# Modulation of a two-layer diffusion backbone on one core: four feature blocks in TensorE's four column tiles, and gate rows through DRAM

## The chip, the cores and the metric

One core of a Trainium2 chip runs the whole program. The metric is the device time of one execution in microseconds, the median of several runs of one build. One execution was also recorded by the hardware profiler, and all rows below come from it.

## The reference, cut to what matters

384 tokens (128 context, 256 latent) of width 1024 go through two layers. Each layer makes six modulation vectors of 1024 for each of two conditioning vectors (context and latent):

```python
def _modulation(cond, w, b):
    m = (jax.nn.silu(cond) @ w + b)[:, None, :]     # w: 1024 x 6144
    return jnp.split(m, 6, axis=-1)

def _layer(x, cond, attend, p, ffn):
    shift_a, scale_a, gate_a, shift_f, scale_f, gate_f = _modulation(cond, p['ada_w'], p['ada_b'])
    h = _ln_plain(x) * (1 + scale_a) + shift_a
    mix, k, v = _token_mixers(h, attend, p)
    x = _ln_affine(DEEPNORM_ALPHA * x + gate_a * mix, p['ln1_g'], p['ln1_b'])
    h = _ln_plain(x) * (1 + scale_f) + shift_f
    x = _ln_affine(DEEPNORM_ALPHA * x + gate_f * ffn(h), p['ln2_g'], p['ln2_b'])
    return x, k, v
```

The mixers are `h @ w_in` (1024 x 2048), attention, a gated convolution and a chunk MLP, then `@ w_out`. The FFN is a dense SwiGLU of width 2816 in layer 0 and the two best of eight experts in layer 1. All is float32.

## The kernel before, in words

Tokens are three tiles of 128. Dense products split both operands into two fp32r parts and make three fp32r matmuls for each 128 of the contraction. Weights arrive by DMA from SyncE's queue in units of 1 MB into five buffers named `st`, and are split by ScalarE (`CAST q<-st`) and VectorE (`TENSOR_TENSOR q<-st,q`) into the buffers `wh` and `wl`. `w_in` comes in four quarters of 512 columns.

A planner (`Plan`) records every operation and then writes each engine's order by itself: it always takes the ready operation with the earliest estimated start, and among those that could start at once the one that the program names first, inside a window of 380 operations. So the order in the text is a priority, not the order of execution. Buffers are given out by tag, in the text's order within a tag. PSUM has eight banks: at most three `pd` (dense sums), two `py` (modulation, and the output sums of the FFN) and three `pm` (transposes, attention). When the plan leaves TensorE idle long enough, `keep_warm` adds matmuls on the identity. `matmuls` records several matmuls as one operation, which the planner can't part.

The modulation of one block `nb` of 512 features (12 a layer; shift_a is 0 and 1, scale_a 2 and 3, gate_a 4 and 5, shift_f 6 and 7, scale_f 8 and 9, gate_f 10 and 11) is `ada_rows`: two units of `ada_w`, each four fp32 matmuls of 128 contraction rows with 32 output columns (two used, the conditioning vectors) in the four column tiles of TensorE. Column tile j holds the sum over contraction blocks j and 4 + j, so rows 32j and 32j + 1 of the bank hold a quarter of the sum. The bank is copied to fp32r `eh` and the rest `el`, and matmuls with a selection matrix add the four quarters: `ada_cols` turns them into feature columns (eight matmuls with `selc`, 128x2), `ada_bcast` into two tiles that hold a row on all 128 partitions (four matmuls with `selb`, 128x512, for the gates), and `ada_dram` into a row that goes to DRAM (two matmuls with `selc` as stationary operand), from where `spread` fetches it for the routing and the end.

The fills lie between the quarters of `w_in` in `mixers` (`fill(0)` to `fill(3)`) and between the two halves of an FFN step (`fill(n)`). Layer 0 makes blocks 0 to 3 at the start, 6 to 9 in fills 0 to 2 (one, one, two blocks), 4 and 5 before the last attention tile, 10 and 11 in FFN steps 2 and 3, and layer 1's 0 to 3 in FFN steps 1 to 4. Layer 1 makes 6 to 11 in fills 0 to 2 and 4 and 5 at the same place.

Of the kernel before, what the change touches and what calls it, by code (L numbers as in the profile page):

```python
# [10 lines left out]
F32 = mybir.dt.float32  # L11
# [9 lines left out]
P = 128  # L21
D = 1024
NT = 3
KC = 8
# [10 lines left out]
FILL0 = ((0,),(1,),(2,3),())  # L35
GATE = 1
# [9 lines left out]
FILL2 = ((0,1), (2,3), (4,5), (), ())  # L46
# [197 lines left out]
class Plan:  # L244
# [36 lines left out]
    def record(self, eng, name, a, k, others=(), more=()):  # L281
# [15 lines left out]
        for b, _ in more:  # L297
            outs.append(b[0])
            ins += b[1:]
# [34 lines left out]
        if more:  # L334
            op.alts[eng] = (name, a, k, self.price(eng, name, outs, list(a[1:]), a, k) + sum(self.price(eng, name, [b[0]], list(b[1:]), b, q) for b, q in more))
# [62 lines left out]
    def flush(self):  # L398
# [85 lines left out]
        for o in order:  # L484
            if not isinstance(o, Op):
                o()
                continue
            a = [x.real() if isinstance(x, (View, Later)) else x for x in o.args]
            if o.name == "call":
                a[0](*a[1:], **{q: v.real() for q, v in o.kw.items()})  # L490
                continue
            k = {q: (x.real() if isinstance(x, View) else x) for q, x in o.kw.items()}
            getattr(self.real[o.eng], o.name)(*a, **k)  # L493
            for b, q in o.more:
                getattr(self.real[o.eng], o.name)(*[x.real() for x in b], **q)  # L495
# [80 lines left out]
class Net:  # L576
    def __init__(self, ctx, nc, tc, A, O):
        self.bnc, self.tc, self.A, self.O = nc, tc, A, O
        self.nc = Plan(nc)
        self.n = 0  # L580
        self.part = ''
        ep = ctx.enter_context
        self.const = ep(tc.tile_pool(name="const", bufs=1))
        sb = ep(tc.tile_pool(name="sb", bufs=1))
        ps = ep(tc.tile_pool(name="ps", bufs=1, space=PSUM))
        self.pools = {}
        dr = ep(tc.tile_pool(name="dr", bufs=1, space=bass.MemoryType.DRAM))
        for pool, name, elems, cap in (
            (dr, "dr", NT * D, dict(dr=1)),
            (dr, "md", 6 * 512, dict(md=1)),  # L590
            (sb, "st", 2048, dict(st=5)),
            (sb, "q4", 1024, dict(x=3, a4=12, wh=6, wl=6)),
            (sb, "q2", 512, dict(m2=21, e2=3)),
            (sb, "q1", 24, dict(s=47)),
            (ps, "bank", 512, dict(pd=3, py=2, pm=3)),
        ):
            p = PPool(pool, name, elems, sum(cap.values()), cap, pool is ps)
            p.cap.update(CAPS.get(name, {}))
            for k in cap:
                self.pools[k] = p  # L600
# [48 lines left out]
    def setup(self):  # L649
# [14 lines left out]
        self.selc = const([2], F32R, "selc")  # L664
        idv = self.idf.rearrange("p (a b) -> p b a", b=32)
        tmp = const([2], F32, "selt")
        nc.vector.tensor_reduce(tmp, idv[:, 0:2, :], axis=AX.X, op=ALU.add)  # L667
        nc.vector.tensor_copy(self.selc, tmp)
        self.selb = const([2, P], F32R, "selb")
        for m in range(2):  # L670
            nc.vector.tensor_copy(self.selb[:, m, :], tmp[:, m : m + 1].to_broadcast([P, P]))
# [58 lines left out]
    def ada_rows(self, l, nb):  # L730
        nc = self.nc
        pa = self.bank([512], name="zrows", tag="py")
        for half in range(2):
            w = self.load(self.A["ada_w"][l, nb, half], 4, 512)
            for j in range(4):
                nc.tensor.matmul(
                    pa[32 * j : 32 * j + 32, :], self.cs[:, 4 * half + j, :], w[:, j, :],
                    start=(half == 0), stop=(half == 1), tile_position=(0, 32 * j),
                )
        eh = self.m2([512], F32R, "eh", tag="e2")  # L740
        el = self.m2([512], F32R, "el", tag="e2")
        nc.any.copy(eh, pa)
        nc.vector.tensor_sub(el, pa, eh.bitcast(F32))
        return eh, el

    def ada_cols(self, l, nb, out, one):

        nc = self.nc
        eh, el = self.ada_rows(l, nb)
        pc = self.bank([4, 2], name="zcols", tag="py")  # L750
        for j in range(4):
            s = slice(128 * j, 128 * j + 128)
            nc.tensor.matmul(pc[:, j, :], eh[:, s], self.selc, start=True, stop=False)
            nc.tensor.matmul(pc[:, j, :], el[:, s], self.selc, start=False, stop=True)
        b = self.abc[:, l, 4 * nb : 4 * nb + 4][:, :, None].to_broadcast([P, 4, 2])
        nc.vector.scalar_tensor_tensor(out, pc, one, b, op0=ALU.add, op1=ALU.add)
        return eh, el

    def ada_dram(self, l, nb, i, one, e=None):

        nc = self.nc
        b = self.m2([512], name="mrow")[0:2]
        nc.sync.dma_start(b, self.A["ada_b"][l : l + 1, 512 * nb : 512 * nb + 512].to_broadcast([2, 512]))
        eh, el = e or self.ada_rows(l, nb)
        pr = self.bank([512], name="zmrow", tag="py")[0:2]
        nc.tensor.matmul(pr, self.selc, eh, start=True, stop=False)
        nc.tensor.matmul(pr, self.selc, el, start=False, stop=True)
        nc.vector.scalar_tensor_tensor(b, pr, one, b, op0=ALU.add, op1=ALU.add)
        nc.sync.dma_start(self.mod[0:2, i, :], b)

    def spread(self, i, m, tag="m2", hold=False):
# [3 lines left out]
        self.nc.sync.dma_start(w.rearrange("p a f -> p (a f)") if n == 2 else w, self.mod[m : m + 1, i : i + n, :].rearrange("p a f -> p (a f)").to_broadcast([P, 512 * n]))  # L775
        return w

    def ada_bcast(self, l, nb, one, out=None):

        nc = self.nc  # L780
        out = out or [self.m2([512], name="mod") for m in range(2)]
        for o in out:
            nc.sync.dma_start(o, self.A["ada_b"][l : l + 1, 512 * nb : 512 * nb + 512].to_broadcast([P, 512]))
        eh, el = self.ada_rows(l, nb)
        for m in range(2):
            pb = self.bank([512], name="zbc", tag="py")
            nc.tensor.matmul(pb, self.selb[:, m, :], eh, start=True, stop=False)
            nc.tensor.matmul(pb, self.selb[:, m, :], el, start=False, stop=True)
            nc.vector.scalar_tensor_tensor(out[m], pb, one, out[m], op0=ALU.add, op1=ALU.add)
        return out  # L790
# [173 lines left out]
    def mixers(self, l, h, fill, ahead, then, ws=None):  # L964
# [66 lines left out]
        gate = lambda: [self.ada_bcast(l, 4 + nb, 0.0) for nb in range(2)]  # L1031
# [6 lines left out]
        ga = gate()  # L1038
# [72 lines left out]
    def ffn(self, l, h, fill, then):  # L1111
# [4 lines left out]
        for n, g in enumerate((5, 0, 1, 2, 3, 4)):  # L1116
# [100 lines left out]
    def route(self, mid):  # L1217

        nc = self.nc
        mods = {(i, m): self.spread(2 * i, m, "a4") for i in range(2) for m in range(2)}  # L1220
# [408 lines left out]
    def moe(self, l, mid):  # L1629
        nc, A, tc = self.nc, self.A, self.tc  # L1630
        self.pools["a4"].cap.update(**CAPS2)
        cnt = self.route(mid)
# [104 lines left out]
    def lead(self, gf, ya):  # L1737
# [4 lines left out]
        for nb in range(2):  # L1742
            gf.append([self.spread(4 + nb, m, hold=True) for m in range(2)])
# [15 lines left out]
    def body(self):  # L1759
# [47 lines left out]
        for g in range(2):  # L1807
            self.ada_cols(0, g, sh[g], 0.0)
            self.ada_cols(0, 2 + g, sc[g], 1.0)
# [3 lines left out]
        self.tables(0)  # L1813
        shf, scf = cols("shf"), cols("scf")

        def fill0(i):
            for n in FILL0[i]:
                self.ada_cols(0, 6 + n, (shf + scf)[n], n // 2)

        hf = []  # L1820
        self.mixers(0, h, fill0, lambda: None, make_h("f", scf, shf, hf), ws)
        sh, sc = cols("sh"), cols("sc")

        def fill1(g):
# [9 lines left out]
        self.mod = self.m2([6, 512], name="mod", tag="md", hold=True)  # L1834

        def fill2(i):
            for n in FILL2[i]:
                one = 1.0 if n in (2, 3) else 0.0
                e = self.ada_cols(1, 6 + n, (shb + scb)[n], one) if n < 4 else None
                self.ada_dram(1, 6 + n, n, one, e)  # L1840

        self.part = '1'
        self.mixers(1, h, fill2, lambda: self.route_prep(scb, shb), lambda t: None)
        self.moe(1, lambda: fill2(4))
# [27 lines left out]
def _layout(I):  # L1872
# [25 lines left out]
    R["ada_w"] = kblk(I["ada_w"], 2, 512)  # L1898
# [51 lines left out]
```

## Time and profile before

| what | value |
|---|---|
| median of three runs | 1175.7 us (1173.18 to 1180.41) |
| profiled execution, own time | 1172.83 us |
| its span, first to last instruction | 1171.1 us |
| mean granted TensorE clock | 0.982 |
| DMA | 282.66 MB, mean 241 GB/s |

The span lies 1.7 us inside the execution's own time, and that execution 2.9 us under the median. In the rows L493 is the one line from which the planner issues nearly all instructions (L495 for the later matmuls of a group of `matmuls`, L510 for the filler), so groups are told apart by their tiles: `st` are loaded units, `cs` the conditioning columns, `q` any SBUF buffer, `bank` any PSUM bank, `md` the DRAM rows, `dr` the routed rows in DRAM. An fp32 matmul shows as two instructions.

### The profile page before, as it was taken

Reading aid. Unit: us, or ns where it says so; the run is one execution under the profiler, and the core shown is the slowest. Engines: PE = TensorE matmul, PEld = TensorE weight load, DVE = VectorE, ACT = ScalarE, POOL = GpSimd, SP = SyncE. Lnnn points to the kernel's source line nnn. Section 1 sums busy time; section 2 is a strip of 40 time slices with the busy share of each in tenths; the row PEclk is TensorE's granted clock in tenths of the full one; section 3 lists DMA queues with packets and bytes.
Section 4 is the critical chain, followed back from the end, with each engine's and each line's share of the span. In section 5 each row is a group of like instructions: output and inputs, shape, how many; then the busy total and the mean of one; then the engine's idle time right before and its main releaser. Section 6 shows DMA issues by size and latency. Waiting matters only on the chain. (4 is left out here: it accounts for less than half of the span.)

```text
span 1171.1 us, 15554 instructions
## 1 busy us (share of the span) xinstructions
PE 1133.1 (97%) x5578; PEld 862.3 (74%) x5578; DVE 827.2 (71%) x1391; ACT 626.4 (53%) x997; POOL 124.3 (11%) x141
## 2 busy tenths in 40 slices
PE   8999999999999999989999899999999999999995
PEld 4666668877777878756666677888888888887673
DVE  4475669443535344797568877999999998987855
ACT  4545547431313223264455326878878786885652
POOL 3430003000000000055000110000000000011201
PEclk8999999999999999999999969999999999999998
DMA  9775544573839465354557436999979997996541
GB/s 375 275 267 197 166 142 143 199 269 139 328 110 332 150 238 197 149 185 156 199 186 268 163 130 224 352 362 361 345 294 347 379 361 297 366 343 245 184 176 58
DMA packets 49398, 282.66 MB, mean 241 GB/s; under 512 B 6312, under 2 KB 8104, under 8 KB 21408
## 3 DMA queue, kind: packets, MB, share of 16 engines
q1 hardware_dynamic: 47056, 275.46, 63.7%
q0 software_dynamic: 1392, 4.55, 1.1%
q10 hardware_dynamic: 864, 1.57, 0.4%
q8 instruction: 46, 0.75, 0.3%
q14 instruction: 40, 0.33, 0.1%
HBM read 278.13 MB, written 3.43 MB: 240 GB/s over the span
## 5 line engine op out<-in xcount | busy, mean ns | idle before, releaser
L493 PE MATMUL bank<-q,q 128*128 128x512 f32 (+4 forms) x4111 | 969.6, 389 | 2.6 <-DVE q L493 1.3
L493 PEld LDWEIGHTS bank<-q,q 128*128 128x128 f32 x4111 | 734.4, 189 | 196.4 <-issue 33.6
L493 DVE TENSOR_TENSOR q<-st,q 128x1024 fp32r<-128x1024 f32 x394 | 453.9, 1178 | 113.4 <-ACT q L493 89.0
L493 ACT CAST q<-st 128x1024 fp32r<-128x1024 f32 x394 | 394.0, 1016 | 196.0 <-PE bank L493 101.3
L493 DVE TENSOR_TENSOR q<-bank,q 128x512 fp32r<-128x512 f32 (+5 forms) x117 | 73.0, 635 | 70.6 <-ACT q L493 57.7
L493 DVE TENSOR_TENSOR q<-q,bank 128x512 f32<-128x512 f32 (+3 forms) x111 | 63.8, 584 | 76.7 <-PE bank L493 69.9
L493 ACT CAST q<-bank 128x512 fp32r<-128x512 f32 (+2 forms) x97 | 53.7, 562 | 103.7 <-PE bank L493 94.0
L493 ACT COPY q<-bank 128x128 f32<-128x128 f32 (+3 forms) x184 | 54.5, 350 | 76.3 <-PE bank L493 67.9
L493 PE MATMUL bank<-idf,q 128*128 128x128 f32 (+1 forms) x502 | 81.7, 287 | 12.9 <-ACT q L493 7.4
L493 POOL TENSOR_TENSOR q<-q,nhalf 128x1 f32<-128x1 f32 (+3 forms) x42 | 42.0, 1005 | 473.8 <-DVE q L493 473.7
L493 PEld LDWEIGHTS bank<-idf,q 128*128 128x128 f32 (+1 forms) x502 | 63.2, 147 | 39.5 <-ACT q L493 12.6
L493 POOL TENSOR_TENSOR q<-q,q 128x512 fp32r<-128x512 f32 (+5 forms) x69 | 61.5, 909 | 216.6 <-ACT q L493 155.0
L493 ACT ACTIVATE q<-bank 128x512 f32<-128x512 f32 (+4 forms) x57 | 29.6, 520 | 81.2 <-PE bank L493 74.4
L493 DVE TENSOR_TENSOR q<-q,q 128x512 f32<-128x512 f32 (+13 forms) x131 | 52.3, 420 | 17.4 <-POOL q L493 8.5
L493 PE MATMUL bank<-st,cs 128*32 128x512 f32 x384 | 54.8, 606 | 0.3 <-DMA st<-in_ada_w_dram 0.3
L272 POOL DMA_INDIRECT q<-dr,q x9 | 14.7, 1638 | 346.3 <-DVE q L493 346.3
L493 ACT ACTIVATE q<-bank,q 128x384 f32<-128x384 f32 (+2 forms) x62 | 33.5, 551 | 24.6 <-DVE q L493 21.5
L493 DVE TENSOR_REDUCE q<-bank 128x1 f32<-128x384 f32 (+5 forms) x64 | 24.5, 411 | 20.8 <-PE bank L495 13.5
L493 DVE SCALAR_TENSOR_TENSOR q<-q,q,q 128x512 f32<-128x512 f32 (+1 forms) x43 | 35.5, 882 | 0.1
L510 PE MATMUL bank<-idr 128*128 128x512 f32 x85 | 30.3, 500 | 1.9 <-DVE selt L667 1.7
L495 PE MATMUL bank<-q,q 64*128 64x384 f32 (+2 forms) x76 | 31.7, 515 | 0.0
L493 ACT ACTIVATE q<-bank,q,q 128x128 f32<-128x128 f32 x70 | 26.6, 467 | 4.6 <-DVE q L493 2.8
(90 smaller groups left out, 395.4 us busy)
## 6 DMA issues: line engine op xcount, KB each, us to landing
st<-in_ada_w_dram SPq DMA_DIRECT2D x48, 1024.0 KB
st<-in_moe_w2a_dram SPq DMA_DIRECT2D x40, 1024.0 KB
st<-in_moe_w1a_dram SPq DMA_DIRECT2D x32, 1024.0 KB
st<-in_moe_w3a_dram SPq DMA_DIRECT2D x32, 1024.0 KB
st<-in_ffn_w_dram SPq DMA_DIRECT2D x22, 1024.0 KB
st<-in_w_in_dram SPq DMA_DIRECT2D x16, 1024.0 KB
st<-in_moe_w1b_dram SPq DMA_DIRECT2D x16, 768.0 KB
st<-in_moe_w3b_dram SPq DMA_DIRECT2D x16, 768.0 KB
```

Source lines behind the costliest of these rows:

```text
L272: self.nc.gpsimd.indirect_dma_start(out=out, out_offset=None, in_=src.rearrange("p t d -> (p t) d"), in_offset=o)
L493: getattr(self.real[o.eng], o.name)(*a, **k)
L495: getattr(self.real[o.eng], o.name)(*[x.real() for x in b], **q)
L510: self.nc.tensor.matmul(z, a, b, start=True, stop=True)
```

## The change

The weights are laid out anew in DRAM. A group is now four feature blocks (2048 features, a third of a layer), and a unit of 1 MB is 128 contraction rows by these 2048 features. The four matmuls of a unit put the four blocks into the four column tiles, so after eight units each tile holds the whole sum of its own block, and nothing is left to add. They are recorded with `matmuls`, as one operation. Columns come from one copy of the bank to SBUF and four 128x128 transposes for a group. Rows (gates, and in layer 1 shift and scale too) are read from the bank by VectorE, two rows a block with the bias added, written to DRAM, and fetched onto all partitions by `spread`; the broadcasting matmuls are gone. The very first group (layer 0, blocks 0 to 3) differs: there two tiles hold the two halves of the contraction for a shift block and two for a scale block, so that four units suffice for each half of the features, and four fp32 matmuls with the selection matrix `selk` (128x4) make the columns.

Placing: each mixer fill 0 to 3 now takes four units in both layers, group 1 (blocks 4 to 7) in fills 0 and 1, group 2 (8 to 11) in fills 2 and 3. FFN steps 1 to 4 take two units each for layer 1's group 0, in one `py` bank that stays held from step 1 to step 4; the column bank moves to `pm` there and in the mixers. The FFN's gates are fetched in step 4, and the two blocks that FFN steps 2 and 3 held are gone from there. The numbers of units (48), of bytes and of fp32 matmuls on them stay.

```diff
...
@@ -332,7 +329,8 @@
         if more:
-            op.alts[eng] = (name, a, k, self.price(eng, name, outs, list(a[1:]), a, k) + sum(self.price(eng, name, [b[0]], list(b[1:]), b, q) for b, q in more))
+            own = lambda b: [v for v in b[1:] if isinstance(v, View)]
+            op.alts[eng] = (name, a, k, sum(self.price(eng, name, [b[0]], own(b), b, q) for b, q in [(a, k), *more]))
...
-            (dr, "md", 6 * 512, dict(md=1)),
+            (dr, "md", 12 * 512, dict(md=2)),
...
+    def ada_group(self, l, n, units, zr=None):
+        nc = self.nc
+        zr = zr or self.bank([512], name="zrows", tag="py")
+        for u in units:
+            w = self.load(self.A["ada_w"][l, n, u], 4, 512)
+            split = (l, n) == (0, 0)
+            first, last = (u % 4 == 0, u % 4 == 3) if split else (u == 0, u == KC - 1)
+            k = [4 * (j % 2) + u % 4 if split else u for j in range(4)]
+            nc.matmuls([(zr[32 * j : 32 * j + 32, :], self.cs[:, k[j], :], w[:, j, :], dict(start=first, stop=last, tile_position=(0, 32 * j))) for j in range(4)])
+        return zr
+
+    def ada_start(self, g, sh, sc):
+        nc = self.nc
+        zr = self.ada_group(0, 0, range(4 * g, 4 * g + 4))
+        e = self.m2([512], name="ae")
+        nc.any.copy(e, zr)
+        pc = self.bank([4, 2, 2], name="zcols", tag="py")
+        for c in range(4):
+            nc.tensor.matmul(pc[:, c].rearrange("p i m -> p (i m)"), e[:, 128 * c : 128 * c + 128], self.selk, start=True, stop=True)
...
+    def ada_out(self, l, n, zr, cols, rows):
+        nc = self.nc
+        if cols:
+            e = self.m2([512], name="ae")
+            nc.any.copy(e, zr)
+            pt = self.bank([4, P], name="zcols")
+            for c in range(4):
+                nc.tensor.transpose(pt[:, c, :], e[:, 128 * c : 128 * c + 128], self.idf)
+            for j, (out, one) in cols.items():
+                nb = 4 * n + j
+                b = self.abc[:, l, 4 * nb : 4 * nb + 4][:, :, None].to_broadcast([P, 4, 2])
+                nc.vector.scalar_tensor_tensor(out, pt[:, :, 32 * j : 32 * j + 2], one, b, op0=ALU.add, op1=ALU.add)
+        if rows:
+            b = self.m2([512], name="mrow")
+            for j, one in rows.items():
+                r, nb = slice(32 * j, 32 * j + 2), 4 * n + j
+                nc.sync.dma_start(b[r], self.A["ada_b"][l : l + 1, 512 * nb : 512 * nb + 512].to_broadcast([2, 512]))
+                nc.vector.scalar_tensor_tensor(b[r], zr[r], one, b[r], op0=ALU.add, op1=ALU.add)
+                nc.sync.dma_start(self.mod[l][0:2, nb, :], b[r])
...
         fill(3)
-        if GATE == 1:
-            ga = [self.ada_bcast(l, 4 + nb, 0.0) for nb in range(2)]
-            gate = lambda: ga
+        ga = [[self.spread(l, 4 + nb, m) for m in range(2)] for nb in range(2)]
         self.attend(2, qT[2], mt[2])
...
-            if n == 2:
-                gf[0] = self.ada_bcast(l, 10, 0.0)
-            elif n == 3:
-                gf[1] = self.ada_bcast(l, 11, 0.0)
+            if n == 4:
+                gf = [[self.spread(l, 10 + nb, m) for m in range(2)] for nb in range(2)]
...
+        def fill(l, sh, sc):
+            z = {}
+            def f(i):
+                if i > 3:
+                    return
+                n, us = 1 + i // 2, range(4 * (i % 2), 4 * (i % 2) + 4)
+                z[n] = self.ada_group(l, n, us, z.get(n))
+                if i == 1:
+                    self.ada_out(l, 1, z[1], {2: (sh[0], 0.0), 3: (sh[1], 0.0)}, {0: 0.0, 1: 0.0} if l == 0 else {0: 0.0, 1: 0.0, 2: 0.0, 3: 0.0})
+                if i == 3:
+                    self.ada_out(l, 2, z[2], {0: (sc[0], 1.0), 1: (sc[1], 1.0)}, {2: 0.0, 3: 0.0} if l == 0 else {0: 1.0, 1: 1.0, 2: 0.0, 3: 0.0})
+            return f
...
         def fill1(g):
             if 1 <= g <= 4:
-                self.ada_cols(1, g - 1, (sh[0], sh[1], sc[0], sc[1])[g - 1], 0.0 if g < 3 else 1.0)
+                z0[0] = self.ada_group(1, 0, (2 * g - 2, 2 * g - 1), z0[0])
+            if g == 4:
+                self.ada_out(1, 0, z0[0], {0: (sh[0], 0.0), 1: (sh[1], 0.0), 2: (sc[0], 1.0), 3: (sc[1], 1.0)}, {})
...
```

## Rows read from the trace of the kernel before

**Rows 1.** The page's first part: busy time of each engine, its share of the span and its instructions.
```profile
PE 1133.1 (97%) x5578; PEld 862.3 (74%) x5578; DVE 827.2 (71%) x1391; ACT 626.4 (53%) x997; POOL 124.3 (11%) x141
```

**Rows 2.** The table by stage: for each stretch (us from the span's start) its length, the busy time of each engine with its instructions, the granted TensorE clock as a share of 2.4 GHz, the busy share of the DMA engines, and GB/s.
```profile
60.00:180.00 120.00, 118.40 (x611) 78.71 (x612) 82.14 (x178) 57.18 (x160) 13.64 (x20) 1.00 0.51 183
180.00:480.00 300.00, 299.16 (x1462) 238.04 (x1461) 147.56 (x194) 108.82 (x146) 13.11 (x11) 1.00 0.59 213
480.00:540.00 60.00, 54.49 (x266) 39.45 (x265) 54.89 (x114) 27.92 (x61) 22.82 (x27) 1.00 0.40 141
540.00:660.00 120.00, 120.00 (x626) 79.05 (x625) 80.83 (x176) 57.55 (x157) 14.71 (x18) 1.00 0.59 213
...
660.00:690.00 30.00, 25.40 (x112) 22.56 (x111) 22.89 (x50) 11.22 (x15) 5.89 (x7) 0.71 0.29 114
```

**Rows 3.** What TensorE waited for from 150 to 480 us: engine and line, the releaser, then us in total, times, longest.
```profile
PE bank L493 <- DVE q L493: 0.4, 1, 0.4
```

**Rows 4.** TensorE's groups of instructions by form: busy us and the mean ns of one, then idle time before them.
```profile
L493 PE MATMUL bank<-selc,q 128*128 128x2 f32 x128 | 16.6, 239 | 2.0 <-ACT q L493 1.1 <-DVE q L493 0.9
...
L493 PE MATMUL bank<-q,q 128*128 128x8 f32 x48 | 10.6, 359 | 0.2 <-ACT q L493 0.2
L493 PE MATMUL bank<-q,selb 128*128 128x512 f32 x24 | 7.6, 399 | 0.0
...
L493 PE MATMUL bank<-q,selc 128*2 128x512 f32 x12 | 4.6, 400 | 1.5 <-DVE q L493 1.5
```

**Rows 5.** TensorE's instructions in order of time, neighbours of one form merged: start, us, engine, line, operation, out and in, count, and idle time before where there was any. The form with `st,cs` is the modulation's product, `selc` and `selb` are its selection matrices, `idf` are transposes, `q,q` dense work.
```profile
43.76 1.02 PE L493 MATMUL bank<-st,cs 128*32 128x512 f32 x2 [0.29 <-DMA st<-in_ada_w_dram]
...
103.33 1.92 PE L493 MATMUL bank<-st,cs 128*32 128x512 f32 x16
...
139.31 1.05 PE L493 MATMUL bank<-st,cs 128*32 128x512 f32 x4
...
140.88 1.91 PE L493 MATMUL bank<-st,cs 128*32 128x512 f32 x12
...
144.14 0.40 PE L493 MATMUL bank<-q,selb 128*128 128x512 f32 x1
144.37 0.39 PE L493 MATMUL bank<-q,q 128*128 128x512 f32 x1
...
244.35 0.60 PE L493 MATMUL bank<-idf,q 128*128 128x128 f32 x4
244.70 5.82 PE L493 MATMUL bank<-q,q 128*128 128x512 f32 x24
...
258.84 0.95 PE L493 MATMUL bank<-selc,q 128*128 128x2 f32 x8
259.65 32.40 PE L493 MATMUL bank<-q,q 128*128 128x512 f32 x139
...
613.02 1.05 PE L493 MATMUL bank<-st,cs 128*32 128x512 f32 x4
```

**Rows 6.** VectorE's and ScalarE's groups by form: busy us, mean ns, idle before.
```profile
L493 DVE TENSOR_TENSOR q<-bank,q 128x512 fp32r<-128x512 f32 x77 | 52.3, 688 | 57.5 <-ACT q L493 57.2
...
L493 DVE SCALAR_TENSOR_TENSOR q<-bank,q 128x512 f32<-128x512 f32 x12 | 7.7, 685 | 1.0 <-PE bank L493 0.8
...
L493 ACT CAST q<-bank 128x512 fp32r<-128x512 f32 x77 | 44.4, 588 | 79.3 <-PE bank L493 69.8 <-PE bank L495 9.5
```

**Rows 7.** The DMA issues of SyncE's queue in order of time, 520 to 545 us, and its waits from 521 to 535 us.
```profile
533.54 0.23 SPq L493 DMA_DIRECT2D md<-q  x1
539.16 0.35 SPq L493 DMA_DIRECT2D st<-in_w_in_dram  x1
...
SPq L493 <- DVE q L493: 17.8, 5, 7.0
```

**Rows 8.** The last modulation units before the experts on TensorE, the stores of the routed rows with the time that a DMA on this tensor took from issue to landing, and an issue of the experts' weights from SyncE's queue.
```profile
621.43 1.92 PE L493 MATMUL bank<-st,cs 128*32 128x512 f32 x16
...
L493 ACTq DMA_DIRECT2D dr<-q x6: 326/380/460, 681.3 to 687.8; - x6
...
DMA to landing us min/median/max: 4.2/7.1/8.5
...
694.88 0.33 SPq L493 DMA_DIRECT2D st<-in_moe_w3a_dram  x1
```

**Rows 9.** Two rows of the table by stage in finer stretches, and single rows of ScalarE, TensorE and SyncE's queue in order of time around the first two fills.
```profile
0.00:30.00 30.00, 24.17 (x113) 13.84 (x113) 12.24 (x34) 12.40 (x22) 9.92 (x24) 0.89 0.93 375
...
40.00:50.00 10.00, 9.71 (x40) 6.02 (x39) 4.36 (x14) 6.19 (x14) 4.38 (x3) 1.00 0.98 403
...
51.07 1.07 ACT L493 CAST q<-st 128x1024 fp32r<-128x1024 f32 x1
...
64.48 11.10 PE L493 MATMUL bank<-q,q 128*128 128x512 f32 x47
...
66.75 11.54 SPq L493 DMA_DIRECT2D st<-in_ada_w_dram  x4
```

**Rows 10.** VectorE's instructions in order of time in an FFN step: the last split of loaded weights, and two additions of output sums.
```profile
255.22 1.23 DVE L493 TENSOR_TENSOR q<-st,q 128x1024 fp32r<-128x1024 f32 x1 [0.17 <-PE bank L493]
...
262.00 0.69 DVE L493 TENSOR_TENSOR q<-q,bank 128x512 f32<-128x512 f32 x1 [2.02 <-PE bank L493]
264.78 0.69 DVE L493 TENSOR_TENSOR q<-q,bank 128x512 f32<-128x512 f32 x1 [2.09 <-PE bank L493]
```

More of the change, by code (lines that the diff above doesn't have):

```diff
@@ L494, in flush @@
             for b, q in o.more:
-                getattr(self.real[o.eng], o.name)(*[x.real() for x in b], **q)
+                getattr(self.real[o.eng], o.name)(*[x.real() if isinstance(x, View) else x for x in b], **q)
     def keep_warm(self, at, order):
@@ L662, in setup @@
         nc.vector.memset(self.nhalf, -0.5)
[L664 to L671, printed above, removed]
+        self.selk = const([4], F32, "selk")
+        idv = self.idf.rearrange("p (i j r) -> p i j r", j=2, r=32)
+        for i in range(2):
+            nc.vector.tensor_add(self.selk[:, 2 * i : 2 * i + 2], idv[:, i, 0, 0:2], idv[:, i, 1, 0:2])
         self.iot = const([P], F32, "iot")
@@ L727, in plain @@
         return out
-    def ada_rows(self, l, nb):
+    def ada_group(self, l, n, units, zr=None):
         nc = self.nc
[L732 to L744, printed above, removed]
@@ L746, in ada_cols @@
-    def ada_cols(self, l, nb, out, one):
-        nc = self.nc
[L749 to L757, printed above, removed]
@@ L759, in ada_dram @@
-    def ada_dram(self, l, nb, i, one, e=None):
-        nc = self.nc
[L762 to L769, printed above, removed]
@@ new lines, in ada_group @@
+        return zr
+    def ada_start(self, g, sh, sc):
+        nc = self.nc
+        zr = self.ada_group(0, 0, range(4 * g, 4 * g + 4))
[4 more added lines that the diff above has]
+            nc.tensor.matmul(pc[:, c].rearrange("p i m -> p (i m)"), e[:, 128 * c : 128 * c + 128], self.selk, start=True, stop=True)
+        for i, (out, one) in enumerate(((sh, 0.0), (sc, 1.0))):
+            nb = 2 * i + g
+            b = self.abc[:, 0, 4 * nb : 4 * nb + 4][:, :, None].to_broadcast([P, 4, 2])
+            nc.vector.scalar_tensor_tensor(out, pc[:, :, i, :], one, b, op0=ALU.add, op1=ALU.add)
@@ L776, in spread @@
         return w
[L778 to L790, printed above, removed]
@@ L1216, in route @@
     @in_mode("route")
-    def route(self, mid):
+    def route(self, l, mid):
         nc = self.nc
-        mods = {(i, m): self.spread(2 * i, m, "a4") for i in range(2) for m in range(2)}
+        mods = {(i, m): self.spread(l, 6 + 2 * i, m, "a4") for i in range(2) for m in range(2)}
         self.lg = self.bank([NT, NE], name="zlogit", tag="py")
@@ L1742, in lead @@
         for nb in range(2):
-            gf.append([self.spread(4 + nb, m, hold=True) for m in range(2)])
+            gf.append([self.spread(1, 10 + nb, m, hold=True) for m in range(2)])
         for t in range(NT):
@@ L1833, in body @@
         shb, scb = cols("shb"), cols("scb")
[L1834 to L1840, printed above, removed]
         self.part = '1'
-        self.mixers(1, h, fill2, lambda: self.route_prep(scb, shb), lambda t: None)
-        self.moe(1, lambda: fill2(4))
+        self.mixers(1, h, fill(1, shb, scb), lambda: self.route_prep(scb, shb), lambda t: None)
+        self.moe(1, lambda: None)
 def _perm():
```

28 lines of the change are left out of this document (12 added, 16 removed).

## The prediction

> **What bounds the kernel now.** I read the page first, then a table by stage, then what TensorE waits for, then its instructions one by one. The page shows PE busy 97% of the span [rows 1], so the question is where PE's time is real work. The table by stage answers it: PE is busy 118.4 of 120 us in the first layer's mixers (60 to 180), 299.2 of 300 in its dense FFN (180 to 480) and 120 of 120 in most of the second layer's mixers (540 to 660), at a granted clock of 1.00, while DMA is busy 0.51 to 0.59 of the time and DVE 82 of 120, 148 of 300 and 81 of 120. [Rows 2] From 150 to 480 PE waited 0.4 us for DVE and next to nothing else. [Rows 3] So there a microsecond of PE work removed is a microsecond of the span, unless something else takes the place. Three stretches are different. The first 60 us begin with loads at 375 GB/s [rows 9] and with filler matmuls on the identity. Between 480 and 540 PE idles 5.5 us and DVE is busy 54.9 of 60: the vector chain of the layer change sets the pace. After 660 come routing and the experts, which the change doesn't touch; whatever is gained before 660 moves them forward as a whole, because their first weights are issued when buffers come free, not by the clock.
>
> **What goes from PE.** Before, the four column tiles hold four quarters of the contraction, so every block of 512 features has to be summed over the tiles by matmuls with a selection matrix. The sixteen blocks made into columns take eight matmuls of 128x2 each; the row forms take 12 matmuls into 2x512 and 24 broadcasting ones into 128x512. Their busy time is 16.6, 4.6 and 7.6 us. [Rows 4] Busy time of pipelined matmuls overlaps, so I price them by the distance from one start to the next. Eight selection matmuls begin at 258.84 and the next work at 259.65, 0.81 us a block. One row matmul holds the place from 144.14 to 144.37, 0.23 us. [Rows 5] That is 16 x 0.81 = 13.0 and 36 x 0.23 = 8.3, together 21.3 us.
>
> The second saving is the bundle. A 1 MB unit is four matmuls, eight instructions in the trace; two whole units in a row (x16, at 103.33) take 1.92 us, 0.96 each. Where the planner put other matmuls in the middle of a unit, each piece costs nearly a whole one: x4 at 139.31 takes 1.05 us and x12 at 140.88 another 1.91, 2.96 for two units, so a break costs 1.0; a single matmul of a unit, x2 at 43.76, takes 1.02. I count seven such breaks, two in the first 60 us, three in the first mixers, two in the second; the first and the last, at 43.76 and 613.02, stand in the rows. [Rows 5] Made one instruction for the planner, a unit can't be broken: 7.0 us.
>
> **What comes to PE.** The five groups that end in columns after the start need 4 transposes each, 20 in all. Four begin at 244.35 and the next work at 244.70, while their own row says 0.60 us [rows 5]: 0.09 to 0.15 each, 1.8 to 3.0 in all. I take 2.5, nearer the upper end, as these wait for a copy and may stand alone. The start needs eight fp32 matmuls with 4 columns. The trace has none; the nearest are the router's fp32 matmuls with 8 columns, two instructions each, 48 in 10.6 us [rows 4], so 16 x 0.22 = 3.5 us, and no less than 16 at the 0.10 us of the selection matmuls, 1.6. I take 3.5. The 48 units stay 48, with the same bytes.
>
> **By stage.** Start: two of the four blocks and half of the fp32 matmuls fall beside filler and cancel; the rest is -1.6 - 2.0 + 1.7 = -1.9 us. First mixers: -3.2 (four blocks) - 1.8 (eight row matmuls) - 3.0 (three breaks) + 1.0 (eight transposes); two gate blocks move here from the FFN, four units, +3.8: -3.2. FFN: -3.2 - 1.8 - 3.8 + 0.5 = -8.3. Second layer's mixers: -3.2 - 20 x 0.23 - 2.0 + 1.0 = -8.8, of which some 2.3 (two blocks and three row matmuls) lie in the DVE-paced stretch, and half of that I don't count: -7.7. The sum is -21.1 us.
>
> **DVE, ACT and PSUM.** Twenty-four fp32r copies (0.59 each) and 24 subtractions (0.69) become 7 copies; 18 row additions (0.69) become 12. [Rows 6] That is some 20 us of DVE and 10 of ACT, hidden under PE except from 480 to 540, where two subtractions and two row additions, 2.7 us, leave the pacing engine. This is an upside of up to 2.7 that I leave to the range.
>
> **What waits more.** Queue first. In the first layer four row writes and eight broadcasts join SP's queue. A row write waits there for its DVE addition, and behind it stand the weight loads; the trace has this already in the second layer: the write at 533.54, and the next weight load behind it at 539.16. [Rows 7] SP's waits in such a stretch are mostly for DVE to free a weight buffer anyway (17.8 us in 521 to 535) [rows 7], so I cost it at nothing; uncovered it is a few us for each of the two groups per layer. The rows of the attention gate are made after the second fill and read after the fourth, with two quarters of w_in between, 2 x 72 x 0.23 = 33 us of dense matmuls; the FFN gate has the whole FFN. In the second layer the scale rows now come from the last fill, whose units ran at 621.4, and the routing wants them when it writes its rows at 681. [Rows 8] Three DMAs lie between. The nearest landing time is that of those routed rows, 4.2 to 8.5 us [rows 8], so 13 to 26 us against 56: hidden.
>
> Loads next. The first and second fill of layer 0 issue four units instead of two ahead of the next quarter of w_in. At 375 GB/s a unit is 2.8 us, so these weights come up to 5.6 us later, twice. Around the first, from 40 to 50, DMA was already busy 0.98, so the delay is real; but the weights were split from 51.1 and their matmuls ran from 64.5 [rows 9], 13 us later, so most of it is covered; I take +1 of 0 to 11.
>
> PSUM last. The group for the second layer's first modulation is accumulated over four FFN steps and holds one of the two "py" banks from step 1 to step 4. The FFN's output sums use the same two banks, and for 18 sums only one is left. Between two sums PE then waits for the DVE addition, 0.69 plus two hops. In the trace sums end every 2.78 us [rows 10], and the last split of what I read as the next step's w1 weights ends at 256.4, before the first sum of the step is read at 262.0. [Rows 10] So 72 dense matmuls (16 us) stand ready in every step to fill five or six gaps of about 0.9 (the hops at 0.1 each, my estimate, as no row has one alone); the planner picks the next ready instruction. I cost it at 0, with 18 x 0.9 = 16 us if the cover fails.
>
> Total: 1172.8 (the profiled execution; its span is 1171.1) - 21.1 + 1 = 1152.7, taken as 1153. That execution is 2.9 us under the median of the three runs, 1175.7, and within their spread of 7; I forecast 1153 all the same, for the upside on DVE. 1% of the median, 11.8 us, is about what a measurement here can tell from no change.
>
> **Rivals.** (a) *One bank, gaps open.* The planner fails to fill, and 18 gaps of 0.9 give 1169. If the gaps also bring the clock down it ends slower: from 660 to 690, with PE 25.4 of 30 busy, the granted clock was 0.71, a mean of its two levels, 1.2 and 2.4 GHz [rows 2]; three steps of 17 us of sums at that clock cost 50 x 0.41 = 20 more: 1189. Against it: 480 to 540 with PE 54.5 of 60 kept 1.00. The point at which it decides is whether PE shows idle time between 255 and 400. The Trainium skill ("TensorE: Matmul & The Clock Gate", A second HAM failure mode) describes just this, micro-idles from cycling PSUM banks that make the clock oscillate; no stretch of before shows it with small gaps. Chance 0.13, 0.08 of it slower than 1% over.
> (b) *Weights late in layer 0's mixers.* Both fills cost their full 5.6 us, and the pending column bank, now among the three "pm" banks that attention uses, holds attention up: 1153 + 10 to 14 = 1165. For it: four units in a row issued from 66.75 took 11.5 us of SP's queue ahead of the next weights. [Rows 9] Chance 0.10.
> (c) *The saved matmuls were not on the path.* In the mixers attention's chain through ACT and DVE could be the real limit, and PE's busy time padded by the model; only the FFN's 8.3 comes through, 1164.5. Against it: dense matmuls stand between all attention steps. Chance 0.10.
> (d) *More comes out than PE's sum*: DVE relief and a better order give 1143 to 1147. I count this inside the forecast.
>
> **How the numbers follow.** Forecast with (d): 0.67, its own range 1142 to 1163. Low end: all of 22, the 2.7 of DVE and 5 for a better order. High end: half of the gain. The range of 8 in 10 takes in (b), (c) and the first half of (a): 1141 to 1173. Faster by over 1% (under 1164): 0.67 plus a third of (b) and (c), 0.73; same: 0.19; slower: 0.08.
>
> **What would show it.** No matmuls on the selection matrices, 20 more 128x128 transposes; every unit x8 or a multiple; PE busy less by some 21 us before the experts with the idle time of 180 to 480 still near 1 us; the experts' first weight load after routing some 20 us earlier than 694.9 [rows 8]; clock 1.00 in the FFN. PE idle behind DVE between 255 and 400 would make (a) right, PE idle at 50 to 110 behind ACT or DVE casts of w_in (b), fewer busy microseconds with an unchanged end of the mixers (c).

## The result and the profile after

The changed kernel takes **1146.3 us**, the median of four runs (1143.41 to 1149.25), beside 1176.6 for the kernel before in the same comparison: a ratio of 0.975 with an interval of 0.972 to 0.978. A second build of the same code (the first experiment) gives 0.9752 (0.9727 to 0.9778). The forecast was 1153 with a range of 1141 to 1173. The profiled execution took 1148.13 us with a span of 1146.4.

The page's first part, after. Columns as in [rows 1].

```profile
PE 1108.2 (97%) x5449; PEld 843.7 (74%) x5449; DVE 814.3 (71%) x1362; ACT 615.4 (54%) x980; POOL 123.8 (11%) x138
```

Against [rows 1] TensorE has 24.9 us and 129 instructions less: 164 selection and broadcasting matmuls are gone [rows 4], 20 transposes and 16 small matmuls (eight in fp32) have come, and the filler has one less. The span is shorter by 24.7. PE's share is 97% on both sides: the engine has become less loaded and no less full.

The table by stage, after. Columns as in [rows 2].

```profile
60.00:180.00 120.00, 120.00 (x628) 80.54 (x627) 84.46 (x178) 59.62 (x165) 18.71 (x20) 0.99 0.55 211
180.00:480.00 300.00, 299.35 (x1433) 240.27 (x1432) 152.35 (x198) 102.37 (x132) 11.59 (x10) 1.00 0.57 206
480.00:540.00 60.00, 55.17 (x277) 37.59 (x275) 50.94 (x106) 31.64 (x64) 27.35 (x32) 0.97 0.54 198
```

The FFN now lies from 187 to 469, and there PE is busy 282.00 of 282.00 us at a granted clock of 1.00; the list of what it waited for is empty in that stretch, where before's had one wait of 0.4 [rows 3].

TensorE's groups by form, after. Columns as in [rows 4]; L491 and L493 together are what L493 was, since the later matmuls of a `matmuls` group come from L493 here.

```profile
L491 PE MATMUL bank<-idf,q 128*128 128x128 f32 x514 | 84.5, 288 | 13.7 <-ACT q L491 7.3 <-DVE q L491 4.5 <-DMA q<-dr,q 1.5
L493 PE MATMUL bank<-st,cs 128*32 128x512 f32 x288 | 48.2, 612 | 0.0
L491 PE MATMUL bank<-st,cs 128*32 128x512 f32 x96 | 47.8, 612 | 0.5 <-DMA st<-in_ada_w_dram 0.4
L491 PE MATMUL bank<-selk,q 128*128 128x4 f32 x16 | 2.0, 249 | 0.3 <-ACT q L491 0.3
```

Nothing on `selc` or `selb` is left. The 384 instructions on `st,cs` are as many as before, and all are in whole units. This is how one looks in order of time (columns as in [rows 5]):

```profile
248.61 0.62 PE L491 MATMUL bank<-st,cs 128*32 128x512 f32 x1
248.62 0.63 PE L493 MATMUL bank<-st,cs 128*32 128x512 f32 x3
249.06 0.59 PE L491 MATMUL bank<-st,cs 128*32 128x512 f32 x1
249.07 0.60 PE L493 MATMUL bank<-st,cs 128*32 128x512 f32 x3
```

Four instructions, one for each column tile, start within 0.01 us of each other and hold TensorE for 0.44 us together; this pair of rows, twice, is a unit (an fp32 matmul is two instructions): 0.88 us with a second unit right behind it; a unit with other work on both sides holds 1.00 (as at 42.61), two in a row 1.85.

**Where the time went, by places on TensorE.** I give each TensorE instruction the distance to the next start, idle time included, as the prediction did for single rows, and add these up from the first instruction to the last dense matmul of the second mixers (it starts at 663.36 before and 640.61 after; the changes are taken before rounding):

| group | before, us | after, us | change |
|---|---|---|---|
| selection and broadcast (`selc`, `selb`) | 23.2 | 0 | -23.2 |
| units (`st,cs`) | 52.8 | 46.6 | -6.1 |
| small matmuls (`selk`) | 0 | 1.7 | +1.7 |
| transposes | 33.1 | 34.9 | +1.8 |
| filler, with the waits behind it | 18.5 | 20.4 | +1.8 |
| the rest, nearly all dense | 534.3 | 535.6 | +1.3 |
| sum | 661.9 | 639.2 | -22.7 |

From there to the first routing matmul (`tok`) before takes 35.0 us and after 31.3, another 3.7 off; the experts then take 472.7 and 474.4, 1.7 back. -22.7 - 3.7 + 1.7 = -24.7.

### The profile page after: what moved, and what is told of

Its sections match the earlier page's. It is cut to its first block, busy times and chain, and to the rows that moved or that the text cites. A ratio compares the mean times of both kernels' runs of the same rounds, so it can differ in the third digit from the quotient of the medians.

```text
span 1146.4 us, 15243 instructions
## 1 busy us (share of the span) xinstructions
PE 1108.2 (97%) x5449; PEld 843.7 (74%) x5449; DVE 814.3 (71%) x1362; ACT 615.4 (54%) x980; POOL 123.8 (11%) x138
## 5 line engine op out<-in xcount | busy, mean ns | idle before, releaser
L491 PE MATMUL bank<-q,q 128*128 128x512 f32 (+4 forms) x4111 | 965.4, 389 | 3.1 <-ACT q L491 2.3
L491 PEld LDWEIGHTS bank<-q,q 128*128 128x128 f32 x4111 | 733.7, 188 | 194.7 <-issue 29.9
L491 DVE TENSOR_TENSOR q<-st,q 128x1024 fp32r<-128x1024 f32 x394 | 455.6, 1182 | 100.4 <-ACT q L491 71.5
L491 ACT CAST q<-st 128x1024 fp32r<-128x1024 f32 x394 | 393.9, 1015 | 207.1 <-PE bank L491 144.6
L491 DVE TENSOR_TENSOR q<-q,bank 128x512 f32<-128x512 f32 (+3 forms) x111 | 63.7, 584 | 85.3 <-PE bank L491 81.9
L491 ACT COPY q<-bank 128x128 f32<-128x128 f32 (+3 forms) x191 | 57.1, 354 | 80.3 <-PE bank L491 57.0
L491 PE MATMUL bank<-idf,q 128*128 128x128 f32 x522 | 85.2, 287 | 14.9 <-ACT q L491 7.3
L491 PEld LDWEIGHTS bank<-idf,q 128*128 128x128 f32 x522 | 66.1, 148 | 43.6 <-ACT q L491 13.4
L491 POOL TENSOR_TENSOR q<-q,nhalf 128x1 f32<-128x1 f32 (+3 forms) x42 | 40.8, 977 | 465.0 <-DVE q L491 464.9
L491 ACT CAST q<-bank 128x512 fp32r<-128x512 f32 (+2 forms) x73 | 39.6, 553 | 92.6 <-PE bank L491 82.1
L491 DVE TENSOR_TENSOR q<-bank,q 128x512 fp32r<-128x512 f32 (+5 forms) x93 | 56.6, 622 | 41.2 <-ACT q L491 29.5
L491 POOL TENSOR_TENSOR q<-q,q 128x512 fp32r<-128x512 f32 (+5 forms) x66 | 62.1, 959 | 202.4 <-ACT q L491 135.7
L491 DVE TENSOR_TENSOR q<-q,q 128x512 f32<-128x512 f32 (+13 forms) x134 | 51.8, 410 | 16.5 <-POOL q L491 10.4
L491 ACT ACTIVATE q<-bank 128x512 f32<-128x512 f32 (+4 forms) x57 | 29.6, 519 | 61.5 <-PE bank L491 54.1
L491 ACT ACTIVATE q<-bank,q 128x384 f32<-128x384 f32 (+2 forms) x62 | 33.4, 549 | 27.9 <-DVE q L491 24.9
L491 PE MATMUL bank<-st,cs 128*32 128x512 f32 x96 | 47.8, 612 | 0.5 <-DMA st<-in_ada_w_dram 0.4
L493 PE MATMUL bank<-st,cs 128*32 128x512 f32 x288 | 48.2, 612 | 0.0
L491 DVE TENSOR_REDUCE q<-bank 128x1 f32<-128x384 f32 (+5 forms) x64 | 24.3, 413 | 29.2 <-PE bank L493 23.3
L491 DVE SCALAR_TENSOR_TENSOR q<-q,q,q 128x512 f32<-128x512 f32 (+1 forms) x43 | 39.8, 976 | 0.1
L493 PE MATMUL bank<-q,q 64*128 64x384 f32 (+2 forms) x76 | 31.7, 515 | 0.0
```

The costliest lines, as they stand in the source:

```text
L493: getattr(self.real[o.eng], o.name)(*[x.real() if isinstance(x, View) else x for x in b], **q)
```

## The experiments

Each was timed beside the kernel before. "Than after" compares medians with the second build, 1145.0 us. The last six ran beside a before of 1174.6 to 1174.9 us, the first four beside one of 1173.9; by the ratios, the four of the six that start from after lose 1.0 to 1.8 us less than their medians say.

**The same code again.**

> The changed kernel once more, beside the next three, for a finer interval. By TensorE's start-to-start distances the change took 23.2 us of selection matmuls and 6.2 us of modulation matmuls away and brought 1.7 us on the new selection matrix and 2.2 us of transposes: 25.5 us net, so a ratio of 0.978 to the kernel before. The rival, that less work on VectorE and ScalarE and a luckier order gave some 5 us more, has 0.974.

1145.03 us (1141.89 to 1145.72). Its experts take 472.1 us in the profile, 2.3 less than in the first build's: a run's share, not the change's.

**Before, with each unit recorded as one operation.**

```diff
-for j in range(4): nc.tensor.matmul(zr[32*j:...], ..., tile_position=(0, 32*j))
+nc.matmuls([(zr[32*j:...], ..., dict(tile_position=(0, 32*j))) for j in range(4)])
```

> The kernel before with the four matmuls of a modulation unit recorded as one operation and nothing else. Its written order has 7 units broken by other matmuls, the bundled order has none. If TensorE's places count one by one: 7 breaks at 0.9 to 1.0 us, 6 to 7 us less than before, ratio 0.994. If a broken unit costs nothing where it lies (its neighbours waited anyway): ratio 1.000.

1169.03 us, ratio 0.9954 (0.9937 to 0.9971): 4.8 us by the medians, 5.4 by the ratio, about a fifth of the whole gain. The places of `st,cs` fall from 52.8 to 48.1, and the last dense matmul of the second mixers starts 4.2 earlier. So unbroken units are worth about 5 us, as a part that needs no new layout.

**After, with the four matmuls recorded one by one.**

> The changed kernel with the four matmuls of a unit recorded one by one. Its written order has 8 broken units. If TensorE's places count one by one: 7 to 8 us more than the changed kernel, ratio to before 0.982 to 0.985. If not: the changed kernel's own ratio.

1147.38 us, ratio 0.9772 (0.9746 to 0.9798): 2.3 us slower than after, with overlapping intervals, where 7 to 8 were expected. The trace has the breaks back, and the places of `st,cs` rise from 46.4 to 54.5:

```profile
42.99 1.02 PE L491 MATMUL bank<-st,cs 128*32 128x512 f32 x2 [0.39 <-DMA st<-in_ada_w_dram]
43.94 1.65 PE L491 MATMUL bank<-q,q 128*128 128x512 f32 x6
45.52 1.05 PE L491 MATMUL bank<-st,cs 128*32 128x512 f32 x4
```

Two instructions, one tile's matmul, hold the place for 0.95 us here, as at 43.76 in [rows 5], where the eight of a whole unit hold 0.88 to 1.00 above. The profiled run was the longest of the five (1150.33), 5.3 us over the second build's; at the last dense matmul it is 6.7 behind that build (645.64 and 638.91), for 8.1 of places. What the breaks cost in time is settled only between this 2.3 and the 5.4 of the experiment above.

**After, with VectorE's and ScalarE's saved work put back.**

```diff
+if u % 2:
+    nc.any.copy(eh, w[:, 0, :])                                  # 24 of 128x512
+    nc.vector.tensor_sub(el, w[:, 0, :], eh.bitcast(F32))
```

> The changed kernel with VectorE's and ScalarE's removed work put back without its use: after every second unit a copy to fp32r of 128x512 and a subtraction of 128x512, 24 of each, reading the loaded unit (the results go nowhere). If the gain is TensorE's alone: within 2 us of the changed kernel. If the relief of VectorE and ScalarE gave the part of the gain beyond TensorE's sum: 3 to 6 us more, most of it between the end of the FFN and the second layer's mixers.

1145.78 us, 0.9770 (0.9744 to 0.9795): 0.8 us slower than after by the medians, 2.1 by the ratios, whose intervals overlap. The relief of VectorE, for which the prediction left up to 2.7 us in its range, gave nothing that is clear of the noise. The profile doesn't say that it is worth nothing: the last dense matmul starts at 641.31, 0.7 and 2.4 later than in the two builds of after, and the way from there to the routing, 28.7 us against 31.3 and 32.2, makes up for it.

**After, with matmuls put back on TensorE.** 192 matmuls of 128x2 on constants, eight after every second unit, that compute nothing that is used.

```diff
+if u % 2:
+    for i in range(8): nc.tensor.matmul(zb[:, 2*i:2*i+2], self.bt, self.idr[:, 0:2], start=True, stop=True)
```

> The changed kernel with eight matmuls of 128x2 in fp32r after every second modulation unit, 192 in all, on constants, without a reader. At the 0.11 us that the selection matmuls held: 21 us of TensorE. If TensorE's places count one by one: 18 to 21 us more than the changed kernel, ratio to before 0.991 to 0.993. If the mixers were bound by attention's chain and not by TensorE: only the eight blocks in the FFN, some 4 to 7 us.

1173.89 us, 0.9987 (0.9973 to 1.0001): 28.9 us slower, the whole gain gone. The group's row:

```profile
L491 PE MATMUL bank<-idr,q 128*128 128x2 f32 x192 | 27.7, 264 | 5.3 <-ACT q L491 5.3
```

Their places sum to 25.0 us. But none of them needs loaded data, and 24 run ahead of all other work of TensorE:

```profile
4.26 5.28 PE L491 MATMUL bank<-idr,q 128*128 128x2 f32 x24 [4.26 <-ACT q L491]
```

These hold 0.21 each, 5.2 together, and stand where the second build has filler alone (1.66 to 8.0); still the first unit starts at 15.82 here, 2.4 later than there, and why is not settled. The other 168 hold 19.9 us, 0.12 each, where before's selection matmuls held 0.11 (14.2 for 128). Between the profiles of this kernel and the second build 22.7 us are there at the last dense matmul (661.62 and 638.91), 1.5 come on the way to the routing matmul and 4.0 in the experts. So up to the last dense matmul it is 19.9 and 2.4 against 22.7, near the expected 18 to 21, and what is beyond that lies behind the mixers. With the experiment before it, this shows that the gain came from TensorE in the main.

**Before, with the six gate blocks through DRAM.**

```diff
-ga = [self.ada_bcast(l, 4 + nb, 0.0) for nb in range(2)]
+for nb in range(2): self.ada_dram(l, 4 + nb, 0, 0.0)
+ga = [[self.spread(l, 4 + nb, m) for m in range(2)] for nb in range(2)]
```

> The kernel before with its six gate blocks made as rows, written to DRAM and fetched onto all partitions, at the places where they were broadcast by matmuls before; all else as before. By TensorE's places 24 matmuls of 0.245 us go and 12 of 0.26 come, 2.8 us less: ratio 0.998. If the way through DRAM, which here is made just ahead of its use, holds the residual or the weight loads up: 3 to 10 us more, with TensorE waiting for VectorE at the end of the mixers.

1166.94 us, 0.9933 (0.9916 to 0.9949): 7.9 us, not 2.8. The gain is not in the places of TensorE: the broadcasts' 5.9 us go, 3.2 of row matmuls come, and the units, more often broken, take 55.8 instead of 52.8, so that the last dense matmul of the second mixers starts at 663.65, 0.3 later than before. It is gained after that: from there to the routing matmul it is 28.2 us, 6.8 less than before.

**Before, with the second layer's two gate blocks alone through DRAM.**

> The kernel before with only the two gate blocks of the second layer's mixers through DRAM (written as rows, fetched onto all partitions) instead of broadcast by matmuls; the first layer is left as it was. It asks where the gain of the four gate blocks and of the change in the last stretch before the experts comes from. Theory 1, the gate rows decide the order: with the second layer's gate off TensorE's and VectorE's way the first routing transposes start about 3 us after the last dense matmul of the mixers, not 9, and the way from there to the routing matmul is 28 to 31 us, not 35; with the 8 broadcasting matmuls gone (8 x 0.23 = 1.8 us, 4 matmuls come, 0.9) the run ends 5 to 9 us earlier than before. Theory 2, that order is a chance of the planner that any edit can flip: the transposes start 9 us after, and the run ends 0 to 2 us earlier.

1168.78 us, 0.9946 (0.9928 to 0.9964): 5.8 us, inside the first theory's bounds, and 28.3 us from the last dense matmul to the routing one. TensorE at the end of the mixers, filler first, then the first routing transposes; before:

```profile
663.60 4.73 PE L510 MATMUL bank<-idr 128*128 128x512 f32 x20
672.68 1.97 PE L493 MATMUL bank<-idf,q 128*128 128x128 f32 x8 [4.35 <-ACT q L493]
```

With the gate rows through DRAM:

```profile
665.34 2.02 PE L510 MATMUL bank<-idr 128*128 128x512 f32 x8
668.97 1.36 PE L493 MATMUL bank<-idf,q 128*128 128x128 f32 x8 [1.60 <-ACT q L493]
```

And after:

```profile
640.85 1.75 PE L508 MATMUL bank<-idr 128*128 128x512 f32 x7
643.80 1.36 PE L491 MATMUL bank<-idf,q 128*128 128x128 f32 x8 [1.21 <-ACT q L491]
```

From the filler to the transposes it is 9.1, 3.6 and 3.0 us. What differs there is VectorE's order. Before, it ends the layer norm of two tiles before the routing's statistics:

```profile
665.19 2.73 DVE L493 SCALAR_TENSOR_TENSOR q<-q,q,q 128x512 f32<-128x512 f32 x4
...
668.88 2.75 DVE L493 SCALAR_TENSOR_TENSOR q<-q,q,q 128x512 f32<-128x512 f32 x4
...
671.62 1.87 DVE L493 BATCH_NORM_STATS2 q<-q 128x6 f32<-128x512 f32 x3
```

After, most statistics come ahead of the last normalisations:

```profile
643.40 1.87 DVE L491 BATCH_NORM_STATS2 q<-q 128x6 f32<-128x512 f32 x3
...
645.82 3.76 DVE L491 SCALAR_TENSOR_TENSOR q<-q,q,q 128x512 f32<-128x512 f32 x4
```

The gate rows are not the whole cause. The kernel with the added matmuls has them through DRAM too, and its transposes start 10.7 us after the filler (672.6 and 661.9). Over all twelve kernels: of the ten with these rows through DRAM, nine have the transposes 2.9 to 3.6 us after the filler and 28.2 to 32.3 us from the last dense matmul to the routing one; this one has 33.8, and the two with broadcasting matmuls (before, and before with unbroken units) have 9.1 and 35.0. So it is the planner's order, which the source of the gate rows mostly turns and one other edit turned back. Why it turns is not settled. Within one order the way still differs by up to 4 us, part of it clock: after and the second build, of the same order, take 31.3 and 32.2 us at a mean granted clock of 0.80 and 0.68.

**After, with the second layer's first group in one FFN step.** The eight units and the held bank are all in step 4.

```diff
-if 1 <= g <= 4: z0[0] = self.ada_group(1, 0, (2*g - 2, 2*g - 1), z0[0])
+if g == 4: z0[0] = self.ada_group(1, 0, range(8))
```

> The changed kernel with all eight units of layer 1's first group in FFN step 4, so that the output sums of steps 1 to 3 have both py banks. If the planner fills the gaps of one bank: the same within 2 us. If one bank costs something: up to 16 us less. Eight units in a row on the loads could cost up to 5 us more, seen as TensorE waiting for a loaded unit.

1156.97 us, 0.9838 (0.9824 to 0.9853): 11.9 us slower than after, more than the 5 that were allowed for. It lies in the FFN (284.3 us from the last statistics of its layer norm to the first after it, 272.6 in after), in this place:

```profile
409.30 0.62 PE L491 MATMUL bank<-st,cs 128*32 128x512 f32 x1 [0.63 <-DMA st<-in_ada_w_dram]
...
412.15 0.62 PE L491 MATMUL bank<-st,cs 128*32 128x512 f32 x1 [0.90 <-DMA st<-in_ada_w_dram]
...
415.40 0.62 PE L491 MATMUL bank<-st,cs 128*32 128x512 f32 x1 [1.28 <-DMA st<-in_ada_w_dram]
...
420.29 1.96 PE L491 MATMUL bank<-q,q 128*128 128x512 f32 x6 [0.52 <-DVE q L491]
```

The first five units fill the five `st` buffers, and while they wait for their turn nothing is loaded (the DMA share is 0.00 from 390 to 400). TensorE eats a unit in 0.9 us, and the last three arrive one every 3 us (409.30, 412.15, 415.40); then the FFN's own weights, queued behind the eight, come late, and dense matmuls wait for their splits. The bank held over four steps was the dearer rival of the prediction; what it buys is that two units at a time hide behind the 216 dense matmuls that lie between one pair and the next (250.46 to 302.13).

**After, with the first layer's units later** (2, 2, 6, 6 instead of 4, 4, 4, 4).

```diff
-n, us = 1 + i // 2, range(4 * (i % 2), 4 * (i % 2) + 4)
+a = (0, 2, 4, 10, 16) if l == 0 else (0, 4, 8, 12, 16)          # fill i takes units a[i] to a[i + 1]
```

> The changed kernel with layer 0's 16 units spread over the four fills as 2, 2, 6, 6 instead of 4, 4, 4, 4, so that the next quarters of w_in are loaded as early as before. If weights came late in the changed kernel: 2 to 8 us less, before the FFN begins. If they didn't: within 2 us.

1154.36 us, 0.9823 (0.9804 to 0.9842): 9.3 us slower, which neither case expected, 8.2 of it already there when the FFN begins (195.3 against 187.1). What PE waited for from 60 to 200 (engine, line, releaser; us, times, longest), then the table by stage from 100 to 180:

```profile
PE bank L491 <- DVE q L491: 4.3, 9, 0.9
PE bank L491 <- ACT q L491: 1.7, 2, 1.3
...
100.00:140.00 40.00, 38.02 (x229) 22.26 (x232) 23.52 (x56) 19.09 (x58) 2.62 (x6) 1.00 0.67 251
140.00:180.00 40.00, 37.30 (x163) 23.62 (x156) 25.12 (x47) 18.32 (x49) 0.00 (x0) 0.87 0.62 222
```

In after the one wait there is 0.2 us, and PE is busy 40.00 of 40.00 in both, at a clock of 1.00. Here the clock may be the larger part: it is 0.74 from 140 to 160, after TensorE had idled 1.3 us up to 144.86 behind ScalarE. At the lower of the two levels, 1.2 GHz, 0.74 is 10 of the 20 us, and half of these, 5 us, is an estimate of the most that it cost.

**After, with them earlier** (`a = (0, 6, 10, 13, 16)`).

> The changed kernel with the sixteen units of the first layer's fills cut 6, 4, 3, 3 instead of 4, 4, 4, 4, so that they come earlier where the late cut came later and lost 8 to 9 us. If the time in that layer is set by how late the units come, 2 to 4 us are gained before the FFN, and this beats the changed kernel. If TensorE, busy 120 of 120 us from 60 to 180, has nothing left to gain there, the time is within 1.5 us of the changed kernel. If the weights of w_in behind the first fill come late now (two units more ahead of them, 5.6 us at the rate of the first 60 us), it is 1 to 6 us slower, with TensorE's idle time at 50 to 80.

1154.43 us, 0.9821 (0.9796 to 0.9846): 9.4 us slower, above all three bounds. The third case's idle time is there, but it is a small part: from 40 to 80 PE is busy 36.2 of 40 us where after has 37.7. More is lost at the start of the FFN:

```profile
180.00:200.00 20.00, 17.79 (x111) 15.11 (x110) 19.96 (x32) 16.84 (x30) 8.05 (x7) 1.00 0.44 159
```

After is busy 19.80 there. At the FFN's end the kernel is 5.4 us behind after's profile, at the routing matmul 4.9, and 2 to 5 more lie in the experts, whose length differs by that much between builds. How earlier units disturb the FFN's start is not settled. Either way from four a fill is dear, and none of these kernels beats the changed one.

## Why the prediction was right, and where it was off

**What bounds the kernel** was right: a place on TensorE is worth its time, nearly one for one. Added matmuls with 19.9 us of places among other work (25.0 with those at the start) moved the last dense matmul by 22.7 us and the end by 28.9; broken units with 8.1 moved it by 6.7, and unbroken ones with 4.6 by 4.2. VectorE's work moved the end by 0.8 to 2.1, inside the noise. Rival (c), saved matmuls off the path, falls with that.

**What goes.** Selection and broadcast: 21.3 forecast, 23.2 measured, since the mean place of each kind is a little longer than the single rows read (0.11 us for the columns and 0.25 for the rows, against 0.10 and 0.23). Broken units: 7.0 forecast from seven breaks, 6.1 measured in places, about 5 in time when only that is done.

**What comes** was priced too high, and this is the main mis-sized term of the sum, 2.5 us together: 3.5 for the `selk` matmuls, which hold 1.7 (0.11 an instruction, at the lower bound of 1.6), and 2.5 for 20 transposes, which add 1.8 (0.09 each, the lower bound again). "Nearer the upper end, as these wait for a copy" was wrong: whatever waited, other work stood in the gap. Net on these four terms: -25.8 against -22.3.

**By stage**, the start gained 2.2 (forecast 1.9), the second mixers from the layer norm's first statistics to their last dense matmul 6.8 (7.7), the FFN from its first matmul to its end 12.6 (8.3). In the FFN 5.1 are selections and broadcasts and 3.7 the four units that left (5.0 and 3.8 forecast); of the rest 2.6 are a filler of four and the waits at its first matmuls, from 198.35 before, which are gone. The first mixers gave 1.2 instead of 3.2: their selections and breaks went as forecast, but dense places and filler grew by some 2.5. The +1 for late weights, of 0 to 11, belongs there, and the trace of after shows them (ScalarE's waits from 40 to 62; before has none for `w_in` there):

```profile
ACT q L491 <- DMA st<-in_w_in_dram: 2.8, 2, 2.3
```

SyncE's queue issues these weights at 49.47, behind the four units, where before issues them at 38.66, and their split, at 51.07 in [rows 9], starts at 55.30. From 50 to 62 TensorE idles 1.6 us behind ScalarE and VectorE, where before idles 0.9, and from 58 to 62 its granted clock is 0.57, where before has 1.00; at that clock the four us lose 1.7, by estimate. The later cut of the fills, 8.2 us in this stretch, is no proof of an edge in the loads, as the clock may make up much of it. To the last dense matmul the sum is -22.7 against -20.1.

**After 660** the step failed: "moves them forward as a whole" left out that the stretch to the routing is ordered anew. It gave 3.7 us in the profiled pair (2.8 with the second build), and 6.8 in the profile of before with two gate blocks changed, whose time fell by 5.8. The prediction's remark that a better order might give 5 was the place for it, but it was put beside VectorE's relief, not to the stretch where order decides. As far as the runs show, this gain is the planner's luck, mostly tied to the source of the gate rows and not to the four blocks in the tiles.

**Rows through DRAM**, priced at nothing, cost nothing that shows: the writes wait on SyncE's queue where it waits anyway (columns as in [rows 7]):

```profile
536.17 2.28 SPq L491 DMA_DIRECT2D md<-q  x3
538.54 0.36 SPq L491 DMA_DIRECT2D st<-in_w_in_dram  x1
540.55 0.23 SPq L491 DMA_DIRECT2D md<-q  x1
```

The write and the next weight load stand 2.4 us apart, 5.6 in [rows 7]. The experts' load that stood at 694.88 in [rows 8] is issued at 668.38.

**One bank** (rival a): refuted by the empty list of waits from 187 to 469 and a clock of 1.00; dense matmuls stood ready for every gap, as the prediction had it. The Trainium skill's case of micro-idles from PSUM cycling ("TensorE: Matmul & The Clock Gate", A second HAM failure mode) is one of idles, and there are none in this stretch; no run here shows what it says. **Late weights** (rival b) came in small: the sign named for it, TensorE idle at 50 to 110 behind the splits of `w_in`, is there with 1.6 us, not with the 10 to 14 of the rival.

**The base.** The forecast was made against the profiled execution, 1172.8, and that lies 3.8 us under the median of its runs here, 1176.6, while the profiled run of after lies 1.9 over its own median. Of the 6.7 us by which 1153 was too high, 4.9 are the terms above, against the profiled run, and 1.9 the place of that run.

## What to carry to other kernels

Where the table by stage shows the first engine full at its full clock, price an edit by places, start to next start, and add them: the sum here came within 3 us in 23, with misses of 2 us either way in single terms. Price the operations that come as carefully as those that go, with the nearest row at the same size, and don't load them with waits unless a row shows that nothing else is ready. Where a planner or a scheduler writes the order, the stretches that are not full can gain or lose several us from any edit: leave that in the range, with their idle time as its size, and keep loads of a large side task spread evenly over the work that hides them.

## What the runs showed of the hardware

A matmul into one 32-column tile that stands alone holds TensorE as long as four of them at once: its two fp32 instructions held 0.95 us, the eight of a whole unit 1.00 when it stands alone and 0.88 with another unit behind it. A tiny matmul is not free: 128x2 and 128x4 instructions hold 0.11 to 0.12 us each in a busy TensorE, so the 128 that did nothing but add four quarters cost 14.2 us. A unit of 1 MB, consumed in 0.9 us, came every 3 us when eight were asked for in one FFN step, and TensorE waited. And short idle times can cost more than themselves: after three of 0.2 to 0.6 us the granted clock was 0.57 from 58 to 62 in the changed kernel, and after one of 1.3 us it was 0.74 from 140 to 160 with the later fills; one of 0.9 us in before, at 60.83, left it at 1.00.
